# Four instead of two blocks of a depthwise convolution on TensorE, as products of 32 channels by four shifts

## The chip, the cores and the metric

The kernel runs on one core of a Trainium2 chip. The metric is the device time of one execution in microseconds (us). Engines are named as in the profile: PE is TensorE's matmul, PEld its weight load, DVE is VectorE, ACT is ScalarE, POOL is GpSimd, SP is SyncE, which issues most transfers.

## The reference, cut to what matters

The reference is a network of 256 tokens by 1024 features in f32: two layers of one block, then two of another. The change touches one mixer of the second block. It projects the tokens to several parts. One part goes through a gate and a causal depthwise convolution of 31 taps over 1024 channels, followed by a layer norm and SiLU; the other part is a state-space product (four-tap convolution, decays, chunked products). Both results are joined and projected.

```python
def conformer_conv(u, w_dw, b_dw, ln_g, ln_b):
    val, gate = jnp.split(u, 2, axis=-1)
    hid = causal_depthwise_conv(val * jax.nn.sigmoid(gate), w_dw, b_dw)   # 31 taps, each channel by itself
    return jax.nn.silu(layer_norm(hid, ln_g, ln_b))

def conv_ssd_mixer(u, w_in, ...):
    proj = u @ w_in
    conv_in, z, xbc, dt_raw = jnp.split(proj, [s0, s1, s2], axis=-1)
    ya = conformer_conv(conv_in, ...)
    yb = mamba2_ssd(z, xbc, dt_raw, ...)
    return jnp.concatenate([ya, yb], axis=-1) @ w_out
```

## The kernel before

Every weight is loaded in units of up to 1 MB by SP into `wr` (or `wxr`). ACT copies it to a rounded half `wh` (L225) and DVE subtracts to get the rest `wl` (L226), 1024 columns at a time. A product of f32 accuracy is three PE products, `wh` by high and low activations and `wl` by high ones (`mm3`, all on L206).

The mixer is `ssm`. Channels lie on partitions: 1024 channels are 8 blocks `f` of 128, and `hp` (named `glu` in the profile) holds for each block 30 zero columns and 256 tokens. `glu_turn(c)` transposes the gated values of blocks 2c and 2c+1 into `hp` and appends their convolutions as tasks.

- `taps(f)`: one ACT instruction (L1728) and 30 DVE instructions (L1730), each of which multiplies a shifted window of 256 columns by a channel's tap and adds it to `hc` (`hcv`). Six blocks go this way, in the queue `conv`.
- `taps_pe(f)`: blocks 1 and 6, in the queue `pconv`. ACT makes a diagonal matrix of 128 by 128 for each tap from the identity (`cdg`, by the copy on L222). PE multiplies each diagonal by the shifted window and sums all 31 in one PSUM tile (`cvq`, L206). One ACT instruction (L1756) adds the bias.

Meanwhile the projections run: `pj` of the parts `c` of xbc, of `glu` and of the gate `zz`. After each half of a weight product, `tick()` advances the queues `conv` and `ssd` by 1.4 steps and `pconv` by 0.65. What is posted there is emitted between the products; a scheduler then settles each engine's order. In `ssd`, `xbc_turn` transposes a block (`xbt`), has POOL zero three columns of a tile `xp` (L1870), copies the block into it on ACT, and runs a four-tap convolution: ACT's scaled copy (L1859) and three DVE instructions (L1861), then SiLU (L1862). `state` scales the results for the state product `stp` (`xdt`, `ssy`, `xds` on DVE). Then come the eight quads of the chunked product (`seg`, `yp`, `yo`). When `ssd` and `pconv` have been drained, `tp` transposes the state-space result, and the output projection `po` begins with that half. The layer norm of the convolution (`mu`, `var`) runs beside it, and the second half of `po` follows.

Small tiles come from pools of fixed size that are reused in turn: `t2` has 8 buffers and `a8` has 12. POOL has no transfer in this kernel; SP and ACT issue all. The modulation at the start (`ada`) is the one place where PE multiplies into quarters: 128 rows by 32 columns, output partitions 0, 32, 64 and 96 in turn, 512 columns each.

Of the kernel before, what the change touches and what calls it, by code (L numbers as in the profile page):

```python
# [11 lines left out]
F32 = mybir.dt.float32  # L12
# [3 lines left out]
OP = mybir.AluOpType  # L16
# [19 lines left out]
def shape_constants():  # L36
    p = np.arange(128)
    cm = np.zeros((128, C_N), np.float32)
    cm[:, C_ID:C_ID + 128] = np.eye(128)
    cm[:, C_TRI:C_TRI + 128] = p[:, None] <= p[None, :]  # L40
    cm[:, C_AFTER:C_AFTER + 128] = p[:, None] > p[None, :]
    cm[:, C_BEFORE:C_BEFORE + 128] = p[:, None] < p[None, :]
    cm[:, C_IOTA:C_IOTA + 128] = p[None, :]
    cq = p % 64
    ck = np.arange(64)
    c0 = np.clip(cq - 8, 0, 48)[:, None]
    cm[:, C_COL:C_COL + 64] = np.where((ck >= c0) & (ck < c0 + 16), 0.0, NEG)
    e = np.arange(8)
    cm[:, C_TIE:C_TIE + 64] = (e[None, :] < e[:, None]).reshape(1, 64)
    od = np.zeros((128, 2, 384), np.float32)  # L50
    t = np.arange(256)
    pos = np.stack([t // 64, t % 64], -1).astype(np.float32)
    inv = (10000.0 ** (-np.arange(16, dtype=np.float32) / 16)).astype(np.float32)
    ang = pos[:, :, None] * inv
    cos, sin = np.cos(ang), np.sin(ang)
    ct = np.stack([cos, cos], 2).reshape(256, 64)
    st = np.stack([-sin, sin], 2).reshape(256, 64)
    for q in range(2):
        rel = t[None, :] - (p[:, None] + 128 * q)
        od[:, q, 0:256] = np.where(np.abs(rel) <= 128, 0.0, NEG)  # L60
        od[:, q, 256:320] = ct[q * 128:(q + 1) * 128]
        od[:, q, 320:384] = st[q * 128:(q + 1) * 128]
    dl = np.zeros((128, 1152), np.float32)
    off = 0
    for q in range(2):
        n = 128 * (q + 1)
        rel = (p[:, None] + 128 * q) - np.arange(n)[None, :]
        for dil, win in ((1, 128), (4, 512), (16, 2048)):
            ok = (rel >= 0) & (rel % dil == 0) & (rel <= win)
            dl[:, off:off + n] = np.where(ok, -rel, -1e33)  # L70
            off += n
    return cm, od.reshape(128, 768), dl
# [81 lines left out]
class Net:  # L154
# [1540 lines left out]
    def ssm(self, x, nxt):  # L1695
        nc, I = self.nc, self.I
        V = nc.vector
        w = I["hyb_w_in_2"][0]
        hp = [self.a8([128, 1536], F32, "glu%d" % i) for i in range(2)]
        cw, pr = hp[0][:, 1144:1392], hp[0][:, 1392:1440]  # L1700
        dks = hp[0][:, 1440:1536].rearrange("p (a b) -> p a b", a=3)
        hp = [t[:, 0:1144].rearrange("p (f t) -> p f t", f=4) for t in hp]
        for i, n in enumerate(("ssm_dt_bias_2", "ssm_a_log_2", "ssm_d_2")):
            nc.scalar.dma_start(pr[:, 16 * i:16 * i + 16], I[n].to_broadcast([128, 16]))
# [2 lines left out]
        taps_in = [self.rows_in([("conv_dw_w_2", (15 * i, 15 + 16 * i), 120 + 8 * i)], self.t2([128, 128], "vrow"))  # L1707
                   for i in range(2)]
        hc = self.a8([128, 8, 256], F32, "hcv")
        on_pe = (1,6)  # L1710
        for i in range(2):
            nc.gpsimd.memset(hp[i][:, :, 0:30], 0.0)
        conv, ssd = Side(1.4), Side(1.4)
        pconv = Side(0.65)
        self.sides = [conv, ssd, pconv]
# [19 lines left out]
        def taps_pe(f):  # L1735

            xx = hp[f // 4][:, f % 4]
            p = self.ps([128, 256], "cvq")

            def diags(j0):  # L1740
                dh = self.t2([128, 4, 128], "cdg")
                for j in range(j0, min(j0 + 4, 31)):
                    c = j * 8 + f
                    self.copy(dh[:, j - j0], self.ident, cw[:, c:c + 1])
                return dh

            nxt = diags(0)
            yield
            for j0 in range(0, 31, 4):
                dh = nxt  # L1750
                if j0 + 4 < 31:
                    nxt = diags(j0 + 4)
                for j in range(j0, min(j0 + 4, 31)):
                    self.mm(p, dh[:, j - j0], xx[:, j:j + 256], j == 0, j == 30)
                yield
            nc.scalar.activation(hc[:, f], p, AF.Identity, bias=self.v("conv_dw_b_2", 0, f))  # L1756
            yield

# [18 lines left out]
        def glu_turn(c, gl):  # L1777
            tp = self.ps([128, 2, 256], "glt")
            for f in range(2):
                for tt in range(2):  # L1780
                    self.tr(tp[:, f, tt * 128:(tt + 1) * 128], gl[tt][:, f * 128:(f + 1) * 128])
            f0 = 2 * c % 4
            self.copy(hp[c // 2][:, f0:f0 + 2, 30:286], tp)
            for f in (2 * c, 2 * c + 1):
                if f in on_pe:
                    pconv.tasks.append(taps_pe(f))
                else:
                    conv.tasks.append(taps(f))
# [17 lines left out]
        p = self.ps([16, 256], "dtp")  # L1806
# [4 lines left out]
        p = self.ps([128, 2, 16], "dtt")  # L1811
# [12 lines left out]
        s = self.sm(32, "ssz")  # L1824
# [85 lines left out]
        for c in (2, 0, 1):  # L1910
            us = self.wunits(lambda r0, r1: [(w[r0:r1, 3072 + c * 512:3584 + c * 512], 512)])
            xb = []
            for tt in range(2):
                p = self.ps([128, 512], "pj")
# [76 lines left out]
        for c in range(2):  # L1991
            us = self.wunits(lambda r0, r1: [(w[r0:r1, 2048 + c * 512:2560 + c * 512], 512)])
            for tt in range(2):
                p = self.ps([128, 512], "pj")
# [218 lines left out]
def build(inputs, stop=None):  # L2213
    import concourse.bacc as bacc
    nc = bacc.Bacc("TRN2", target_bir_lowering=False, num_devices=1)
    arrays, args = {}, {}
    consts = dict(zip(("k_cm", "k_od", "k_dl"), shape_constants()))
    col = np.arange(64)
    rel = np.clip(col[None, :] - col[:, None] + 15, 0, 30)
    consts["k_rpb"] = np.asarray(inputs["ev_rpb"])[0][:, 4:11][:, :, rel].transpose(0, 2, 1, 3)  # L2220
    for name in [n for n in _INS if n != "ev_rpb"] + list(consts):
        a = np.ascontiguousarray(inputs[name] if name in inputs else consts[name])
        arrays[f"in_{name}_dram"] = a
        args[name] = nc.dram_tensor(f"in_{name}_dram", a.shape, mybir.dt.from_np(a.dtype), kind="ExternalInput").ap()
    out = nc.dram_tensor("out_0_dram", (1, 256, 1024), F32, kind="ExternalOutput").ap()
    with tile.TileContext(nc) as tc:
        with ExitStack() as ctx:
            Net(ctx, tc, args, out, stop).run()
    return nc, arrays
# [7 lines left out]
```

## Time and profile before

| | us |
|---|---|
| runs (three) | 2501.82, 2499.31, 2494.11 |
| median | 2499.31 |
| profiled execution, its own time | 2498.09 |
| its span, first to last instruction | 2496.3 |
| mean granted PE clock | 0.984 |
| PE busy | 2383.6 (95%) |
| DVE busy | 1812.5 (73%) |
| ACT busy | 1299.0 (52%) |
| POOL busy | 13.0 (1%) |

The profiled execution is one run of the program; its span leaves out 1.8 us around it. Matmuls are pipelined: a record lasts longer than the distance to the next, so what a product costs is the distance between starts. An f32 product leaves two records in the profile. The mixer's part that is touched runs from about 1500 to 1757 us.

### The profile page before, as it was taken

The numbers are of one execution on the slowest core, as the hardware profiler recorded it, in microseconds if no ns is written. First come the engines' busy times: TensorE is split into PE (matmuls) and PEld (weight loads), VectorE is DVE, ScalarE is ACT, GpSimd is POOL, SyncE is SP. The second block draws the span as 40 slices with busy tenths as digits, with TensorE's granted clock in tenths as the row PEclk, the third lists the DMA queues.
The fourth block names the chain that finished last, engine by engine and source line by source line (L and its number), as shares of the span: only waits on it lengthen the run. The fifth ranks groups of instructions, "written<-read, shape, count | busy, mean of one in ns | idle before, by whom it ended". The sixth has DMA issues, their size and how long they took to land.

```text
span 2496.3 us, 32333 instructions
## 1 busy us (share of the span) xinstructions
PE 2383.6 (95%) x11882; PEld 1981.9 (79%) x11882; DVE 1812.5 (73%) x3515; ACT 1299.0 (52%) x2230; POOL 13.0 (1%) x27
## 2 busy tenths in 40 slices
PE   7999999999899879999999999989999999999998
PEld 5878888888788658787877887877788788898886
DVE  5798988676686778989988556998744754646644
ACT  4445333232454568777776445775644544655533
POOL 0000000000000000000000000000000000000000
PEclk9999999999998999999999999999999999999999
DMA  8344455654221159999997654333665555554561
GB/s 275 115 133 163 152 186 190 215 163 166 75 81 56 55 170 321 331 324 338 313 352 264 194 189 144 102 102 126 220 199 172 186 185 167 146 153 136 191 196 51
DMA packets 381471, 455.15 MB, mean 182 GB/s; under 512 B 16680, under 2 KB 313337, under 8 KB 381305
## 3 DMA queue, kind: packets, MB, share of 16 engines
q1 hardware_dynamic: 375481, 445.86, 55.1%
q10 hardware_dynamic: 5824, 7.15, 0.9%
q8 instruction: 95, 1.56, 0.3%
q14 instruction: 71, 0.58, 0.1%
HBM read 451.91 MB, written 1.05 MB: 181 GB/s over the span
## 4 chain that ended last, share of the span: by engine, by line
PE 51%; DVE 7%; ACT 2%; DMA 2%; issue 1%; DVEq 0%; SPq 0%; ACTq 0%
PE gu L206 26%; PE acc L206 13%; PE pj L206 6%; DVE wl L226 3%; DMA wxr<-in_moe_w_dram 1%; DVE hcv L1730 1%; PE ht L209 1%; PE cvq L206 1%; PE po L206 1%; ACT wh L225 1%; PE oat L206 1%; DVE wxl L226 0%; PE mgp L206 0%; DVE c L1861 0%; PE pT L209 0%
## 5 line engine op out<-in xcount | busy, mean ns | idle before, releaser
L226 DVE TENSOR_TENSOR wl<-wr,wh 128x1024 fp32r<-128x1024 f32 (+1 forms) x510 | 590.9, 1186 | 168.7 <-ACT wh L225 167.7
L225 ACT ACTIVATE wh<-wr 128x1024 fp32r<-128x1024 f32 (+1 forms) x510 | 503.3, 1025 | 284.2 <-PE gu L206 55.9
L226 DVE TENSOR_TENSOR wl<-wxr,wh 128x1024 fp32r<-128x1024 f32 (+1 forms) x122 | 144.2, 1207 | 49.6 <-ACT wh L225 44.9
L566 DVE SCALAR_TENSOR_TENSOR aacc<-wr,sc,aacc 128x512 f32<-128x512 f32 x224 | 162.0, 761 | 14.6 <-DMA wr<-in_ada_w_dram 13.6
L206 PE MATMUL gu<-wh,xh 128*128 128x512 f32 x416 | 163.8, 394 | 2.6 <-ACT xh L229 2.6
L206 PE MATMUL gu<-wh,xl 128*128 128x512 f32 x416 | 162.9, 392 | 0.7 <-DVE xl L230 0.7
L206 PE MATMUL gu<-wl,xh 128*128 128x512 f32 x416 | 162.5, 391 | 0.0
L206 PE MATMUL gu<-wl,mgh 128*128 128x512 f32 (+1 forms) x384 | 146.3, 381 | 8.1 <-DVE wl L226 8.1
L225 ACT ACTIVATE wh<-wxr 128x1024 fp32r<-128x1024 f32 (+1 forms) x122 | 123.7, 1043 | 54.2 <-PE acc L206 13.9
L206 PE MATMUL gu<-wh,mgh 128*128 128x512 f32 (+1 forms) x384 | 144.9, 377 | 1.3 <-ACT wh L225 1.2
L226 DVE TENSOR_TENSOR wxl<-wr,wxh 128x1024 fp32r<-128x1024 f32 (+1 forms) x94 | 110.0, 1182 | 46.8 <-ACT wxh L225 43.7
L206 PE MATMUL gu<-wh,mgl 128*128 128x512 f32 (+1 forms) x384 | 143.1, 373 | 0.6 <-DVE mgl L226 0.6
L206 PE MATMUL acc<-wh,hid 128*128 128x512 f32 x416 | 135.3, 396 | 0.0
L435 ACT ACTIVATE sg<-gu,ry 128x256 f32<-128x256 f32 x88 | 41.2, 472 | 164.0 <-PE gu L206 158.8
L225 ACT ACTIVATE wxh<-wr 128x1024 fp32r<-128x1024 f32 (+1 forms) x94 | 95.0, 1024 | 43.4 <-PE acc L206 20.2
L436 DVE SCALAR_TENSOR_TENSOR sg<-gu,ry,sg 128x256 f32<-128x256 f32 x88 | 42.0, 480 | 103.8 <-ACT sg L435 103.8
L206 PE MATMUL acc<-wh,hh 128*128 128x512 f32 x352 | 115.9, 399 | 1.1 <-ACT wh L225 1.1
L206 PE MATMUL gu<-wxh,xh 128*128 128x512 f32 x288 | 113.6, 395 | 1.7 <-ACT xh L229 1.6
L206 PE MATMUL gu<-wxh,xl 128*128 128x512 f32 x288 | 113.2, 393 | 1.4 <-DVE ri L286 0.8
L206 PE MATMUL gu<-wxl,xh 128*128 128x512 f32 x288 | 113.0, 392 | 0.0
L206 PE MATMUL pj<-wh,xh 128*128 128x512 f32 (+1 forms) x248 | 96.9, 392 | 0.6 <-ACT xh L229 0.6
L206 PEld LDWEIGHTS gu<-wh,xh 128*128 128x128 f32 x416 | 78.3, 188 | 20.5 <-ACT xh L229 4.7
(548 smaller groups left out, 5847.0 us busy)
## 6 DMA issues: line engine op xcount, KB each, us to landing
wr<-in_ffn_w_dram SPq DMA_DIRECT2D x176, 512.0 KB
wr<-in_moe_w_dram SPq DMA_DIRECT2D x124, 512.0 KB
wr<-in_ffn_w_dram SPq DMA_DIRECT2D x45, 1024.0 KB
wr<-in_ada_w_dram SPq DMA_DIRECT2D x42, 1024.0 KB
wr<-in_moe_w_dram SPq DMA_DIRECT2D x28, 1024.0 KB
wxr<-in_ffn_w_dram SPq DMA_DIRECT2D x44, 512.0 KB
wxr<-in_moe_w_dram SPq DMA_DIRECT2D x40, 512.0 KB
wr<-in_attn_w_qkv_dram SPq DMA_DIRECT2D x54, 256.0 KB
```

What stands on the lines that cost most here:

```text
L206: self.nc.tensor.matmul(out, lhsT, rhs, start=start, stop=stop)
L209: self.nc.tensor.transpose(out, in_, self.ident)
L225: self.nc.scalar.activation(h, src, AF.Copy)
L226: self.split_op = self.nc.vector.tensor_sub(l, src, h.bitcast(F32))
L435: nc.scalar.activation(g, p[:, 0:n], AF.Silu, scale=rs[tt])
L436: nc.vector.scalar_tensor_tensor(g, p[:, n:2 * n], rs[tt], g, op0=OP.mult, op1=OP.mult)
L566: self.nc.vector.scalar_tensor_tensor(a[:, s], w, col, a[:, s], op0=OP.mult, op1=OP.add)
L1730: V.scalar_tensor_tensor(a, xx[:, j:j + 256], tap(j), a, op0=OP.mult, op1=OP.add)
```

## The change

Blocks 1, 3, 6 and 7 go to PE, and each in another form. A block of 128 channels is cut into four groups `g` of 32 channels. A tile `shifted` (`cxs`) of 128 partitions by 4 groups by 284 columns holds, for group g, the 32 channels four times, shifted by 0, 1, 2 and 3 columns. It is filled by 16 transfers on chip of 32 partitions each, issued by POOL: 64 for the four blocks. A product then takes 128 partitions, which are 32 channels by 4 shifts, and 32 output columns into a quarter of the PSUM tile. Eight products (`r`) with windows 4 columns apart make 32 taps, the last one zero; 4 groups by 8 are 32 products a block. The weights `cdg` come from the taps, laid out on the host as `k_cw`, by two POOL products a block instead of ACT's copies. There is one `shifted` tile for all four blocks.

```diff
+        cq = hp[1][:, 1144:1432]
+        nc.scalar.dma_start(cq, I["k_cw"])
...
-        on_pe = (1,6)
+        on_pe = (1, 3, 6, 7)
         for i in range(2):
             nc.gpsimd.memset(hp[i][:, :, 0:30], 0.0)
+        shifted = self.a8([128, 4, 284], F32, "cxs")
+        nc.gpsimd.memset(shifted[:, :, 283:284], 0.0)
...
             xx = hp[f // 4][:, f % 4]
+            eye = cq[:, None, 256:288].to_broadcast([128, 16, 32])
+            dw = [self.t2([128, 4, 4, 32], "cdg") for _ in range(2)]
+            for i in range(2):
+                c = f * 32 + i * 16
+                nc.gpsimd.tensor_tensor(dw[i].rearrange("p r g c -> p (r g) c"), eye,
+                                        cq[:, c:c + 16, None].to_broadcast([128, 16, 32]), op=OP.mult)
+            for s in range(4):
+                for g in range(4):
+                    n = 284 if s < 3 else 283
+                    nc.gpsimd.dma_start(shifted[32 * s:32 * s + 32, g, 0:n], xx[32 * g:32 * g + 32, s:s + n])
+            for _ in range(6):
+                yield
             p = self.ps([128, 256], "cvq")
-
-            def diags(j0):
...
-            for j0 in range(0, 31, 4):
-                dh = nxt
-                if j0 + 4 < 31:
-                    nxt = diags(j0 + 4)
-                for j in range(j0, min(j0 + 4, 31)):
-                    self.mm(p, dh[:, j - j0], xx[:, j:j + 256], j == 0, j == 30)
-                yield
+            for r in range(8):
+                for g in range(4):
+                    self.mm(p[32 * g:32 * g + 32], dw[r // 4][:, r % 4, g], shifted[:, g, 4 * r:4 * r + 256], r == 0, r == 7)
+                if r % 2:
+                    yield
```

The change also moves instructions. POOL first, from the two memsets of `hp` on; `glu_17573` is `hp[0]` and `glu_17574` is `hp[1]`, which also holds the taps. Before:

```order
L1520 COMPARE_AND_BRANCH
L1520 UNCONDITIONAL_BRANCH x2
L1712 MEMSET glu_17573 128x4x30
L1712 MEMSET glu_17574 128x4x30
L1870 MEMSET xp 128x3 x12
```

After (lines are two to four higher):

```order
L1716 MEMSET cxs 128x4
L1746 TENSOR_TENSOR cdg<-glu_17574 128x512 x2
L1751 DMA cxs<-glu_17573 32x284 x12
L1751 DMA cxs<-glu_17573 32x283 x4
L1874 MEMSET xp 128x3 x9
L1751 DMA cxs<-glu_17573 32x284 x2
L1874 MEMSET xp 128x3
L1751 DMA cxs<-glu_17573 32x284 x10
L1751 DMA cxs<-glu_17573 32x283 x4
L1874 MEMSET xp 128x3 x2
L1746 TENSOR_TENSOR cdg<-glu_17574 128x512 x2
L1751 DMA cxs<-glu_17574 32x284 x2
```

All twelve `xp` memsets stand behind block 1's 16 transfers, one of them also behind two of block 3's and two behind all of block 3's; the transfers of blocks 6 and 7 follow.

PE, from the last quads of the state-space part to the output projection. Before:

```order
L206 MATMUL yo<-st,bcT 128x512
L206 MATMUL yp<-xdt,mm 128x64 x4
L206 MATMUL cvq<-glu_17574,cdg 128x256 x4
L206 MATMUL yp<-xdt,mm 128x64 x4
L206 MATMUL yo<-st,bcT 128x512
L206 MATMUL cvq<-glu_17574,cdg 128x256 x19
L209 MATMUL tp<-cm,xs 128x128 x16
L206 MATMUL po<-wh,ybh 128x512
```

After:

```order
L206 MATMUL yo<-st,bcT 128x512
L206 MATMUL yp<-xdt,mm 128x64 x4
L206 MATMUL cvq<-cxs,cdg 32x256 x8
L206 MATMUL yp<-xdt,mm 128x64 x4
L206 MATMUL yo<-st,bcT 128x512
L206 MATMUL cvq<-cxs,cdg 32x256 x59
L209 MATMUL tp<-cm,xs 128x128 x2
L206 MATMUL cvq<-cxs,cdg 32x256 x29
L209 MATMUL tp<-cm,xs 128x128 x14
L206 MATMUL po<-wh,ybh 128x512
```

All 96 products of blocks 3, 6 and 7 (8, 59 and 29) have come to stand here; block 1's 32 stand between the projections earlier.

## Rows read from the trace of the kernel before

**Rows 1.** The page: busy time by engine, and the chain's shares.

```profile
PE 2383.6 (95%) x11882; PEld 1981.9 (79%) x11882; DVE 1812.5 (73%) x3515; ACT 1299.0 (52%) x2230; POOL 13.0 (1%) x27
...
PE 51%; DVE 7%; ACT 2%; DMA 2%; issue 1%; DVEq 0%; SPq 0%; ACTq 0%
```

**Rows 2.** Stretches (from:to, length): busy by engine, granted PE clock, DMA share, GB/s.

```profile
1560.00:1570.00 10.00, 10.00 (x52) 8.41 (x51) 9.12 (x25) 8.69 (x16) 0.20 (x2) 1.00 0.06 9
...
1630.00:1640.00 10.00, 4.38 (x10) 2.00 (x8) 10.00 (x22) 3.70 (x7) 0.00 (x0) 0.83 0.00 1
...
1690.00:1700.00 10.00, 6.79 (x25) 5.64 (x25) 10.00 (x34) 5.72 (x19) 0.00 (x0) 0.83 0.19 59
```

**Rows 3.** Timeline of PE: start, length, instructions [idle before, and what ended it].

```profile
1589.14 0.38 PE L209 MATMUL xbt<-cm,xb 128*128 128x128 f32 x2
...
1636.63 2.05 PE L206 MATMUL stp<-xds,btm 128*128 128x512 f32 x2 [5.62 <-DVE xds L1895]
1637.69 1.42 PE L206 MATMUL pj<-wh,xh 128*128 128x512 f32 x1
1638.90 1.37 PE L206 MATMUL stp<-xds,btm 128*128 128x512 f32 x2
```

**Rows 4.** Timeline of PE at the last convolution products of block 6.

```profile
1688.11 1.89 PE L206 MATMUL cvq<-glu,cdg 128*128 128x256 f32 x8
1693.21 8.43 PE L206 MATMUL cvq<-glu,cdg 128*128 128x256 f32 x30 [3.21 <-ACT cdg L222]
1701.48 1.91 PE L209 MATMUL tp<-cm,xs 128*128 128x128 f32 x16
```

**Rows 5.** Instructions of the tile `cdg`: count, ns min/median/max, first and last start.

```profile
L206 PE MATMUL cvq<-glu,cdg x124: 377/379/631, 1567.4 to 1701.3; 128*128 128x256 f32 x124
L222 ACT ACTIVATE cdg<-cm,glu x62: 384/387/401, 1554.7 to 1696.9; 128x128 f32<-128x128 f32 x62
```

**Rows 6.** Timeline of PE in the modulation at the start.

```profile
38.73 3.64 PE L206 MATMUL ada<-adw,scw 128*32 128x512 f32 x32
```

**Rows 7.** Timeline of DVE: taps of one block, back to back.

```profile
1568.06 3.65 DVE L1730 SCALAR_TENSOR_TENSOR hcv<-glu,hcv 128x256 f32<-128x256 f32 x9
```

**Rows 8.** Timeline of POOL, three of its instructions.

```profile
2.69 0.23 POOL L516 TENSOR_TENSOR sel<-cm 128x2 f32<-128x2 f32 x1 [1.65 <-DMA cm<-in_k_cm_dram]
...
56.13 2.39 POOL L863 TENSOR_TENSOR bias<-bias,cm 128x1024 f32<-128x1024 f32 x1 [49.77 <-DMA bias<-in_k_rpb_dram]
...
1561.20 0.10 POOL L1870 MEMSET xp<- 128x3 f32 x1 [59.75 <-PE glt L209]
```

**Rows 9.** Timeline of DVE around POOL's product of 56.13.

```profile
55.23 0.94 DVE L226 TENSOR_TENSOR wl<-wr,wh 128x768 fp32r<-128x768 f32 x1
...
56.42 2.91 DVE L226 TENSOR_TENSOR wl<-wr,wh 128x768 fp32r<-128x768 f32 x1
```

**Rows 10.** Timeline of SP: time that issuing a transfer took (64, 24 and 1024 KB).

```profile
0.74 0.39 SPq L319 DMA_DIRECT2D cm<-in_k_cm_dram  x1
...
18.35 1.30 SPq L354 DMA_DIRECT2D vrow<-in_ada_b_dram  x1
...
1525.57 0.37 SPq L254 DMA_DIRECT2D wxr<-in_hyb_w_in_dram  x1
```

**Rows 11.** Timeline of ACT at the first blocks' copies and the first `xp`.

```profile
1561.43 0.59 ACT L222 ACTIVATE glu<-glt 128x512 f32<-128x512 f32 x1
...
1572.89 0.51 ACT L1859 ACTIVATE c<-xp,vec 128x256 f32<-128x256 f32 x1
...
1574.59 1.28 ACT L1862 ACT_TABLE_LOAD   x1
...
1579.93 1.06 ACT L225 ACTIVATE wh<-wxr 128x1024 fp32r<-128x1024 f32 x1 [1.18 <-PE pj L206]
```

**Rows 12.** The chain in order of time: start, length, what.

```profile
1574.11 2.79 PE pj L206 x12
```

More of the change, by code (lines that the diff above doesn't have):

```diff
@@ L1737, in taps_pe @@
             xx = hp[f // 4][:, f % 4]
-            p = self.ps([128, 256], "cvq")
-            def diags(j0):
-                dh = self.t2([128, 4, 128], "cdg")
-                for j in range(j0, min(j0 + 4, 31)):
[L1743 to L1747, printed above, removed]
-            yield
-            for j0 in range(0, 31, 4):
-                dh = nxt
-                if j0 + 4 < 31:
-                    nxt = diags(j0 + 4)
-                for j in range(j0, min(j0 + 4, 31)):
-                    self.mm(p, dh[:, j - j0], xx[:, j:j + 256], j == 0, j == 30)
-                yield
+            eye = cq[:, None, 256:288].to_broadcast([128, 16, 32])
[10 more added lines that the diff above has]
+                yield
+            p = self.ps([128, 256], "cvq")
+            for r in range(8):
[3 more added lines that the diff above has]
+                    yield
             nc.scalar.activation(hc[:, f], p, AF.Identity, bias=self.v("conv_dw_b_2", 0, f))
@@ L2219, in build @@
     rel = np.clip(col[None, :] - col[:, None] + 15, 0, 30)
+    taps = np.zeros((32, 1024), np.float32)
+    taps[0:31] = np.asarray(inputs["conv_dw_w_2"])[0]
+    consts["k_cw"] = np.concatenate([taps.reshape(8, 4, 8, 4, 32).transpose(1, 4, 2, 0, 3).reshape(128, 256),
+                                     np.tile(np.eye(32, dtype=np.float32), (4, 1))], 1)
     consts["k_rpb"] = np.asarray(inputs["ev_rpb"])[0][:, 4:11][:, :, rel].transpose(0, 2, 1, 3)
```

## The prediction

> **What bounds the kernel now.** I read the first part of the page and its chain of waits first [rows 1]: TensorE (PE) is busy for 95% of the span and carries 51% of the chain. Any stretch is therefore priced by asking when PE gets through it. The change touches one mixer, so I took the stretch table of 1560 to 1702 us next [rows 2]. There VectorE (DVE) is as full as PE. Between 1630 and 1640 us PE runs only 4.38 of 10 us, and between 1690 and 1700 us only 6.79. The timeline of PE names both gaps. A state product waits 5.62 us for DVE's `xds` [rows 3], and the last convolution products wait 3.21 us for ScalarE's (ACT's) diagonals [rows 4]. Each gap also costs clock. After the second one, 30 products take 8.43 us, while 8 take 1.89 us before it (0.216 us from one to the next, so 30 would take 6.6) [rows 4]. A wait thus costs about 1.8 us beyond itself, and the granted clock of those stretches is 0.83 instead of 1.00 [rows 2], the mean of a part at 1.2 GHz after the idle time and the rest at 2.4.
>
> **The change, part by part.**
>
> *PE.* Before, two blocks issue 124 records [rows 5] at 0.216 us, which is 27 us. After, four blocks of 32 products issue 256 records (an f32 product leaves two). A row of the same form is in the trace: the modulation products `ada`, 128 rows by 32 columns into four quarters in turn, 32 records of 512 columns in 3.64 us [rows 6], or 0.107 us each after the fill. At 256 columns that is half, 0.0535 us, so 256 records are 13.7 us. PE gives up **13.3 us**.
>
> *The two old gaps.* Block 3's and block 7's 60 taps leave DVE. Nine taps take 3.65 us [rows 7], so they are 60 x 0.40 = 24 us. The 62 diagonals leave ACT [rows 5]. With them go the 5.62 us and the 3.21 us, and a clock loss of 1.8 us each (less for the first, whose products run only some 3 us at the low clock, 1.6): **12.2 us** at most, nothing at least. I take all of it, since the engine that was late loses more work than the gap.
>
> *GpSimd's (POOL's) eight diagonal products.* They are new there and DVE feels them. While POOL's two-input product of 1024 columns runs 2.39 us from 56.13 [rows 8], DVE's subtraction of 768 columns takes 2.91 us instead of 0.94 [rows 9]. This is what the Trainium skill, "SBUF — State Buffer", section "SBUF: two separate sides", states: a GpSimd operation and a VectorE operation that reads two SBUF inputs exclude each other for a whole instruction. By that rule, and the trace agrees, eight products of half that size (1.2 to 1.3 us) take up to 10 of the 24 us back from DVE. That leaves 14, still more than the gap.
>
> *The 64 transfers.* They are the price that decides. They go through POOL's queue, and the order shows three facts. POOL waits with a block's transfers until the block before has been multiplied, because there is one `shifted` tile. The multiplications of blocks 3, 6 and 7 stand in one run at the end of the state-space part, before the output projection. And the twelve small `xp` memsets of POOL, 0.10 us each [rows 8], now stand behind transfers.
>
> No row shows a transfer issued by POOL. SP takes 0.37 us for one of 1 MB and 1.30 us for a small one of 48 rows, 24 KB [rows 10]. Those are my two ends, 0.37 and 1.30 us. By rows, 32 of 48 make 0.87 of the dear one. Each of these transfers also waits for a semaphore that the eighth before it used. I take **1.0 us**, nearest to the dear row. The Trainium skill, "DMA: Bandwidth & Descriptors", section "Latency and other measured facts", names about 1 us for the first byte of a GpSimd transfer; by that price the sum would be the one below. Landing: the first constant is issued at 0.74 us and POOL gets it at 2.69 us [rows 8, 10], 1.6 us after its issue ended. I take 2.0, since weights share the engines.
>
> *First new wait.* Block 1's transfers can start when ACT has copied its rows, at 1562.0 us [rows 11]. Sixteen end at 1578.0, and the first `xp` memset runs then. ACT would reach the scaled copy that needs it near 1571.4 (1572.89 before [rows 11], less one group of convolution products ahead on PE). ACT is in order: behind that copy stand the copies out of PSUM and the weight halves `wh`. From 1578.0 it needs about 8.1 us to the copy `xb` that PE's next transposes read (four scaled copies, a table load of 1.28 and two halves of 1.06 [rows 11], the other copies at 0.3 to 0.7). PE had those transposes at 1589.14 [rows 3]; four groups earlier, at 1.7 us each, is 1582.4. PE waits about **4 us**.
>
> *Second.* When block 1 has been multiplied, block 3's 16 transfers start. One memset stands behind the first two, and two behind all sixteen. The first costs PE 1.5 us. By the last, PE has 46 projection products ahead, 10.7 us at 0.233 [rows 12]. ACT needs 2.5 us behind the memset, so 16 + 2.5 - 1.5 - 10.7 = **6.3 us**. Together the new waits are 12 us; at 0.37 us a transfer they are 1, at 1.30 they are 21.
>
> *The tail.* Block 3's products are the last that have their data when PE gets to them. Block 6's 16 transfers follow them, with two diagonal products of 1.3 us in the same queue: 16 + 2.6 + 2.0 = 20.6 us. Then PE multiplies, and block 7's transfers follow: 16 + 2.0 = 18.0 us. Nothing is queued on PE that could go ahead; the transposes for the output projection stand behind. **38.6 us** (18.4 at 0.37; 48.2 at 1.30), and 2 x 1.8 = 3.6 us of clock after the two waits.
>
> *The sum* is -13.3 - 12.2 + 12 + 38.6 + 3.6 = +28.7 us. The profiled execution took 2498.1 us, 1.2 below the median of the runs. That gives 2526.8 us, **2527**. The norm of the convolution and the output projection behind the tail are PE-bound before, so the shift passes through them.
>
> **The rivals.**
>
> *A cheap issue: not slower.* If POOL issues as quickly as SP issues its weights, 0.37 us, the memsets come in time and the tail shrinks to 18.4 us. The sum is -13.3 - 12.2 + 1 + 18.4 + 3.6 = -2.5 us, 2495.6. For it speaks that SP's rows are mostly the cheap ones; against it, that SP's small transfer is the dear one. The point at which this becomes "no change" is 0.65 us a transfer (sum +7.5). The Trainium skill, "DMA: Bandwidth & Descriptors", section "Issuing engines are not separate DMA queues", says that initiating a DMA is usually small relative to the DMA itself. By that rule this rival holds; no run here shows it yet for POOL. Faster than 2491 needs under 0.28 us, or more gaps of PE closed than the two.
>
> *A dear issue.* Past 1.30 us, or with landing slower than 2.0 us under the weights' traffic, the result is 2545 to 2550 and beyond: the sum at 1.30 is -13.3 - 12.2 + 21 + 48.2 + 3.6 = +47.3. For it: POOL writes the transfers itself while DVE excludes it at times [rows 9].
>
> *The quarters don't overlap: the change doesn't do what it says.* If a product of 32 columns takes PE as long as one of 128, 256 records at 0.216 are 55 us, 42 more than summed: 2568. Against it stands the row of `ada` [rows 6].
>
> **How the numbers follow.** Forecast 2527, with an issue of 0.65 to 1.3 us: 0.64. Cheap issue: 0.18, of which 0.04 reach faster. Dear issue: 0.13. No overlap: 0.05. From the cheap bound, 2496, to the dear one with slow landing, 2550, some 2 in 10 are left out. A measurement of this kernel tells 0.3%, 7.5 us, from no change. Faster is 0.04, the same 0.14, slower 0.82.
>
> **What would show it.** In the profile after, POOL's queue should show 64 transfers in four runs of 16, each 12 to 18 us long, and the stretch of 1560 to 1700 should be near 28 us longer. PE should have two idle gaps of 18 to 21 us with only the products of block 6 between them, waiting for DMA, and the granted clock should fall after each. ACT's scaled copies of `xp` should wait for POOL. The 8-record groups of `cvq` should take near 0.43 us. It is wrong if the transfers take under 0.65 us, if the two gaps are under 10 us, or if PE's waits sit elsewhere than before `cvq`.

## The result, and the profile after

The changed kernel takes 2514.8 us (median), the kernel before 2497.1 (median of five runs, the three of the table above among them). The medians differ by 17.7 us; the ratio is 1.0061, 95% interval 1.0046 to 1.0076, or 15 us more. The forecast was 2527, slower, in a range of 2496 to 2550. The sign held. The price on which the prediction let it hang did not: a transfer takes half of what was assumed, and other terms made up part of the difference.

The profiled execution spans 2513.3 us, 17.0 more than before. Two points of TensorE's (PE's) timeline cut this up: the transposition `dtt` at the mixer's start, and the transposition `tp` of `res` behind the output projection. Before, they stand at 1554.85 and 1754.83 us, 199.98 apart. After:

```profile
1553.53 0.29 PE L1817 MATMUL dtt<-cm,dtr 16*128 16x16 f32 x2 [0.46 <-ACT dtr L222]
...
1767.06 1.03 PE L209 MATMUL tp<-cm,res 128*128 128x128 f32 x8
```

That is 213.53 apart: **the mixer costs 13.5 us more**. Ahead of it 1.3 us were gained, and behind it 4.7 lost (746.2 instead of 741.5 to the end), both with unchanged work. The loss behind sits in one place, some 530 us behind the mixer, where the same products run at a lower granted clock. First the stretches of before, then of after, which lie 13 us later (columns as in [rows 2], the clock third from the end):

```profile
2280.00:2290.00 10.00, 9.48 (x65) 8.67 (x64) 3.05 (x6) 3.92 (x12) 0.00 (x0) 0.93 0.57 212
2290.00:2300.00 10.00, 9.95 (x47) 7.63 (x45) 6.42 (x18) 5.73 (x14) 0.00 (x0) 1.00 0.00 1
```

```profile
2290.00:2300.00 10.00, 8.91 (x46) 8.51 (x47) 4.58 (x7) 5.29 (x14) 0.00 (x0) 0.61 0.59 205
2300.00:2310.00 10.00, 9.48 (x37) 7.93 (x37) 1.00 (x3) 1.08 (x4) 0.00 (x0) 0.70 0.17 54
```

The other profiles below fall on either side too, 740.8 to 741.5 or 746.0 to 747.0 us behind the mixer, whatever they change. So single profiles are compared by their mixer stretch here, and kernels by their medians.

Now the mixer. Busy times on the page, which answer to [rows 1]: POOL has gone from 13.0 to 57.9 us, PE is as busy as before, although its products are cheaper.

```profile
PE 2383.9 (95%) x12014; PEld 1975.0 (79%) x12014; DVE 1790.1 (71%) x3455; ACT 1281.3 (51%) x2168; POOL 57.9 (2%) x100
```

The stretches that answer to [rows 2]:

```profile
1630.00:1640.00 10.00, 8.88 (x46) 7.14 (x45) 9.93 (x19) 5.98 (x13) 0.00 (x0) 1.00 0.58 211
...
1660.00:1670.00 10.00, 10.00 (x54) 9.17 (x54) 8.00 (x15) 6.00 (x13) 0.00 (x0) 0.79 0.03 10
...
1680.00:1690.00 10.00, 0.00 (x0) 0.00 (x0) 7.78 (x19) 1.59 (x5) 8.69 (x15) 0.73 0.85 247
1690.00:1700.00 10.00, 7.16 (x64) 3.51 (x64) 0.00 (x0) 0.17 (x1) 3.85 (x6) 0.58 0.10 23
```

PE's timeline at the places of [rows 3, 4]:

```profile
1626.74 1.12 PE L206 MATMUL stp<-xds,btm 128*128 128x512 f32 x2 [1.42 <-ACT btm L222]
...
1656.77 1.81 PE L206 MATMUL seg<-cm,lt 128*128 128x128 f32 x8 [2.53 <-ACT lt L222]
...
1677.01 2.80 PE L206 MATMUL cvq<-cxs,cdg 128*32 128x256 f32 x48
1692.63 7.16 PE L206 MATMUL cvq<-cxs,cdg 128*32 128x256 f32 x64 [12.82 <-DMA cxs<-glu]
1707.52 2.01 PE L206 MATMUL cvq<-cxs,cdg 128*32 128x256 f32 x6 [7.73 <-DMA cxs<-glu]
1709.46 0.69 PE L209 MATMUL tp<-cm,xs 128*128 128x128 f32 x2
1710.08 4.57 PE L206 MATMUL cvq<-cxs,cdg 128*32 128x256 f32 x58
1714.58 1.75 PE L209 MATMUL tp<-cm,xs 128*128 128x128 f32 x14
```

The reader is to see four things. The state product comes 10 us earlier than in [rows 3] (8.6 if counted from `dtt`), and its gap is 1.42 instead of 5.62. From `dtt` to the end of the last `yo` PE needs 123.6 us instead of 133.4, so it enters the tail 9.9 us ahead. Then two gaps, 12.82 and 7.73 us, are followed by products at half speed: the 64 records of block 6 take 7.16 us, where 48 take 2.80 just before. And a wait that the prediction did not name, 2.53 us for ACT's `lt`, is followed by a granted clock of 0.79. The kernel before waited for `lt` too, in two shorter waits, with a granted clock of 1.00 from 1640 to 1660:

```profile
1648.24 0.49 PE L206 MATMUL seg<-cm,lt 128*128 128x128 f32 x2 [1.53 <-ACT lt L222]
...
1658.01 0.49 PE L206 MATMUL seg<-cm,lt 128*128 128x128 f32 x2 [1.08 <-ACT lt L222]
```

What POOL does in the tail, and the row of its 64 transfers (issue time, minimum/median/maximum):

```profile
1680.36 1.03 POOL L1751 DMA_DIRECT2D cxs<-glu  x2 [60.49 <-issue]
1681.41 2.06 POOL L1746 TENSOR_TENSOR cdg<-glu 128x512 f32<-128x512 f32 x2
1683.40 5.67 POOL L1751 DMA_DIRECT2D cxs<-glu  x11
1691.28 1.47 POOL L1751 DMA_DIRECT2D cxs<-glu  x3 [2.21 <-DMA cxs<-glu]
...
1699.67 7.93 POOL L1751 DMA_DIRECT2D cxs<-glu  x16 [4.85 <-PE cvq L206]
```

```profile
L1751 POOL DMA_DIRECT2D cxs<-glu x64: 496/496/677, 1561.4 to 1707.1; - x64
...
DMA to landing us min/median/max: 1.7/1.7/6.1
```

A transfer takes **0.50 us** to issue, not 1.0. It has landed 1.7 us after its issue began, but up to 6.1 while weights fill the DMA engines (share 0.85 from 1680 to 1690): there POOL waits 2.21 us for a transfer before it can issue three more.

### The profile page after: what moved, and what is told of

It reads as the page before. It is cut to its first block, busy times and chain, and to the rows that moved or that the text cites. A ratio compares the mean times of both kernels' runs of the same rounds, so it can differ in the third digit from the quotient of the medians.

```text
span 2513.3 us, 32590 instructions
## 1 busy us (share of the span) xinstructions
PE 2383.9 (95%) x12014; PEld 1975.0 (79%) x12014; DVE 1790.1 (71%) x3455; ACT 1281.3 (51%) x2168; POOL 57.9 (2%) x100
## 3 DMA queue, kind: packets, MB, share of 16 engines
HBM read 452.06 MB, written 1.05 MB: 180 GB/s over the span
## 4 chain that ended last, share of the span: by engine, by line
PE 49%; DVE 7%; issue 4%; DMA 2%; ACT 2%; POOL 1%; SPq 0%; DVEq 0%; ACTq 0%; POOLq 0%
PE gu L206 26%; PE acc L206 12%; PE pj L206 5%; DVE wl L226 3%; PE po L206 2%; PE ht L209 1%; DVE hcv L1734 1%; DMA wr<-in_moe_w_dram 1%; PE oat L206 1%; DMA wxr<-in_moe_w_dram 1%; ACT wh L225 1%; DVE c L1865 1%; POOL cxs L1751 0%; PE mgp L206 0%; DVE wxl L226 0%
## 5 line engine op out<-in xcount | busy, mean ns | idle before, releaser
L566 DVE SCALAR_TENSOR_TENSOR aacc<-wr,sc,aacc 128x512 f32<-128x512 f32 x224 | 160.1, 752 | 14.5 <-DMA wr<-in_ada_w_dram 13.5
L225 ACT ACTIVATE wxh<-wr 128x1024 fp32r<-128x1024 f32 (+1 forms) x94 | 95.0, 1024 | 43.5 <-PE acc L206 20.3
```

The lines of the kernel that those rows point to most:

```text
L225: self.nc.scalar.activation(h, src, AF.Copy)
L566: self.nc.vector.scalar_tensor_tensor(a[:, s], w, col, a[:, s], op0=OP.mult, op1=OP.add)
```

## The experiments

The theory: block 6's and block 7's transfers each begin only when the block before has left the one `shifted` tile, and at that point PE has nothing else queued. The rivals: the transfers, the diagonal products or their queue cost wherever they stand; the loss sits ahead of the tail; or the products are slow by themselves. "Mixer" is from `dtt` to `tp` of `res`, "tail" from the end of the last `yo` to the first `po`, both of the profiled execution; the ratio is to the kernel before, timed on the same chip.

| kernel | median us | ratio [95%] | mixer | tail |
|---|---|---|---|---|
| before | 2497.1 | | 199.98 | 14.9 |
| changed | 2514.8 | 1.0061 [1.0046, 1.0076] | 213.53 | 39.0 |
| no_transfers_6_7 | 2482.4 | 0.9943 [0.9921, 0.9966] | 187.53 | 11.3 |
| two_tiles | 2498.9 | 1.0007 [0.9995, 1.0019] | 202.58 | 28.0 |
| three_tiles | 2478.2 | 0.9916 [0.9898, 0.9933] | 182.63 | 14.5 |
| early_products | 2493.7 | 0.9992 [0.9980, 1.0004] | 194.62 | 9.9 |
| split_transfers | 2526.9 | 1.0119 [1.0088, 1.0150] | 228.84 | 50.7 |
| issue_from_sp | 2512.7 | 1.0063 [1.0043, 1.0083] | 214.47 | 39.9 |
| keep_warm | 2521.5 | 1.0097 [1.0073, 1.0120] | 225.14 | 50.6 |
| keep_warm_sized | 2506.9 | 1.0034 [1.0017, 1.0050] | 210.23 | 35.7 |
| po_first | 2506.4 | 1.0044 [1.0023, 1.0065] | 211.89 | 12.7 |
| lt_on_pool | 2514.8 | 1.0070 [1.0047, 1.0094] | 214.30 | 37.8 |
| two_blocks | 2498.4 | 1.0000 [0.9988, 1.0011] | 206.10 | 12.0 |

### Do the transfers of blocks 6 and 7 cost it?

```diff
             for s in range(4):
                 for g in range(4):
                     n = 284 if s < 3 else 283
-                    nc.gpsimd.dma_start(shifted[...], xx[...])
+                    if f < 4:
+                        nc.gpsimd.dma_start(shifted[...], xx[...])
```

> Leaves out the transfers of blocks 6 and 7; their products read what block 3 left in the tile. Everything else is the same, GpSimd's diagonal products included. Theory: the gaps of 12.82 and 7.73 us go, and the products of both blocks run at full clock (3.5 us each instead of 7.16 and 6.6): PE reaches the output projection near 1689.5 instead of 1716.1, 2488 (2484 to 2493). So all that the change gains elsewhere shows by itself: 9 us against the kernel before. Rival (the slowdown sits elsewhere, in the waits for VectorE and ScalarE before 1680 us or behind 1716 us): 2500 or more.

Measured 2482.4, below the expectation, and a mixer 26.0 us shorter than the changed kernel's. PE's timeline has all three blocks in one piece, 0.055 us a record:

```profile
1673.20 9.70 PE L206 MATMUL cvq<-cxs,cdg 128*32 128x256 f32 x176
```

So the loss is in these 32 transfers and what follows on them. Without them the change is worth 12.5 us in the mixer.

### Is it the one tile?

```diff
-        shifted = self.a8([128, 4, 284], F32, "cxs")
+        shifts = [self.a8([128, 4, 284], F32, "cxs%d" % i) for i in range(2)]
...
+            shifted = shifts[on_pe.index(f) % 2]
```

> Two shifted tiles in turn instead of one; the order on TensorE (PE) is unchanged. Theory (the single tile makes the transfers of blocks 6 and 7 serial): block 6's transfers run near 1640 us, long before they are needed, so the gap of 12.82 us and the half clock after it (7.16 - 3.6) go, 16.4 us; block 7's transfers still wait for block 3's products, so the gap ahead of them grows from 7.73 to about 10 us. 14 us less than the changed kernel: 2501 (2497 to 2505). Rival (PE is late for GpSimd's diagonal products or for the weights' traffic, not for the tile): the gap stays, 2515.

Measured 2498.9, as expected, and no different from the kernel before (the interval holds 1). The gap ahead of block 6 is down to 2.42 us and waits for its diagonals; the one ahead of block 7, which still shares block 3's tile, has grown to 9.71:

```profile
1678.17 3.97 PE L206 MATMUL cvq<-cxs,cdg 128*32 128x256 f32 x64 [2.42 <-POOL cdg L1748]
1691.86 1.39 PE L206 MATMUL cvq<-cxs,cdg 128*32 128x256 f32 x6 [9.71 <-DMA cxs<-glu]
```

Then three tiles, with `range(3)` and `% 3`, so that no transfer waits for a late block.

> Three shifted tiles: blocks 1 and 7 share one, blocks 3 and 6 have their own; all 64 transfers stay. On GpSimd the transfers of blocks 6 and 7 then stand behind the last xp memset, near 1640 us, with the quads beside them, and PE's order ends with 88 products in a row. Theory (only the wait for the tile costs): both gaps go, up to 3 us come back where the diagonal products of blocks 6 and 7 wait for a small tile: 2486 (2482 to 2492), below the kernel before and near the run without these transfers (2482.4). Rival (32 transfers in a row beside the weights' traffic and the quads cost as much elsewhere): 2497 or more.

Measured **2478.2 us, 0.84% faster than before**, with all 64 transfers in place. POOL issues blocks 6 and 7 from 1637 us on, beside the quads, and PE goes through its products without a gap:

```profile
1637.05 4.43 POOL L1753 DMA_DIRECT2D cxs<-glu  x9 [16.44 <-ACT lt L222]
...
1654.30 2.93 POOL L1753 DMA_DIRECT2D cxs<-glu  x6 [0.27 <-DMA cxs<-glu]
```

```profile
1657.57 0.49 PE L206 MATMUL seg<-cm,lt 128*128 128x128 f32 x2 [0.97 <-ACT lt L222]
...
1674.41 9.70 PE L206 MATMUL cvq<-cxs,cdg 128*32 128x256 f32 x176
1686.04 1.09 PE L209 MATMUL tp<-cm,xs 128*128 128x128 f32 x8 [1.92 <-DVE xs L132]
```

The tail is 24.5 us shorter than the changed kernel's. Another 6.4 us go ahead of it, from `dtt` to the last `yo` (117.2 instead of 123.6): the wait of 2.53 us for `lt` and the low clock after it are not there. These 6.4 us are not a wait for the tile. The scheduler also settled another order on ACT. In the changed kernel ACT turns from the quads to the gate `zz` and back just ahead of the late `lt` of 1656.33, and each turn loads another function table, 1.28 us:

```profile
1652.47 1.28 ACT L2000 ACT_TABLE_LOAD   x1
1653.83 0.69 ACT L2000 ACTIVATE zz<-pj,ry 128x512 f32<-128x512 f32 x1
1654.54 1.28 ACT L1952 ACT_TABLE_LOAD   x1
```

With three tiles the `zz` stand behind the quads, ACT loads no table between the first `mm` of the quads and the last (four in the changed kernel), and the whole program has 12 table loads instead of 16:

```profile
1666.93 1.28 ACT L2002 ACT_TABLE_LOAD   x1
```

No run has this order with one tile, so the share of the loads is read from the two traces and not tested by itself. The profiled mixer is 17.4 us shorter than before's; the rest of the 21 us that the ratio gives is not seen there.

### Or the order of the products?

`pconv = Side(0.65)` becomes `Side(2.0)`, with one tile.

> One number: the convolution tasks on PE advance at 2.0 steps per half of a weight product instead of 0.65; still one shifted tile and 64 transfers. Block 3's products then stand between the projections and block 6's between the quads, so each block's transfers have other PE work beside them. Theory (what costs is that the transfers of two blocks lie behind the last work of PE, not that there are 64 of them): both gaps and their half clock go, PE gets to the transposes near 1687 instead of 1714 us: 2488 (2484 to 2495), below the kernel before. At most 2 us come back where block 1's first products reach PE before its transfers have landed. Rival (GpSimd's queue and its lock on VectorE cost wherever they stand): the waits move ahead, 2505 to 2515.

Measured 2493.7, above the 2488 and within the range, but not clear of the kernel before (the interval holds 1); the tail is the shortest of all, with waits of 0.69 and 0.86 us for transfers. But PE now also waits 3.0 us for them ahead of the tail, and the products stand in smaller groups there: from `dtt` to the last `yo` it takes 134.1 us, 10.5 more than the changed kernel, where the 112 records that have moved ahead of it would be 6.2 at 0.055. Moving the products takes the tail away, but not for nothing; another tile does it better.

The other way round, the output projection's first half goes ahead of the waiting products:

```diff
-        pconv.drain()
         for tt in range(2):
             yb.b(tt)
...
-        conv.tasks.append(norm())
-        conv.rate = 3
+        pconv.tasks.append(norm())
+        pconv.rate = 3
```

> One shifted tile and all transfers as in the changed kernel, but the convolution tasks of PE need not be finished before the transposes and the output projection: its first half is put ahead of and between the products of blocks 6 and 7, and the norm follows them. Theory (the gaps cost because nothing that PE could do stands ahead of them): the waits fill with output products, the half clock goes too: 2489 (2484 to 2497). Rival (the norm, which needs blocks 6 and 7, comes so much later that the second half of the projection waits for it): 2500 or more.

Measured 2506.4, so the rival's bound held. The gaps for transfers have gone (0.33 us are left), and two others stand in their place, on the norm of the convolution and on the transposes' input. PE's waits from 1650 to 1770 us:

```profile
PE po L206 <- ACT yah L225: 7.3, 1, 7.3
PE tp L209 <- DVE rt L301: 6.3, 1, 6.3
```

### What does a transfer cost?

Each is cut into two of half the columns, the same bytes in all.

> Each transfer on chip is cut into two of half the columns, same bytes: 128 instead of 64. Theory (the issue of 0.50 us in GpSimd's queue is the price): a block's run grows from 8 to 16 us, the two tail gaps by 8 us each, and the early waits that the prediction worked out at 1.0 us a transfer appear, up to 12 us: 2531 to 2543. That is the prediction's price of 16 us a block put to the test; its own sum was 2527. Rival (the bytes or the landing set the time): 2515.

Measured 2526.9, some 4 us under the theory's lower end and 12 above the rival. The issue stays at 0.496 us for half the bytes, so a block's run doubles and the gaps become 18.67 and 13.86:

```profile
1706.33 6.79 PE L206 MATMUL cvq<-cxs,cdg 128*32 128x256 f32 x64 [18.67 <-DMA cxs<-glu]
1726.98 2.00 PE L206 MATMUL cvq<-cxs,cdg 128*32 128x256 f32 x4 [13.86 <-DMA cxs<-glu]
```

```profile
L1752 POOL DMA_DIRECT2D cxs<-glu x128: 496/496/698, 1565.3 to 1728.2; - x128
```

This is the prediction's own case, 16 us a block, and the mixer is 28.9 us longer than before, where it summed 28.7. That the sums agree is partly luck. The gaps are 32.5 instead of 38.6, and the early waits far less than 12: from `dtt` to the last `yo` the split costs 3.6 us. ACT's timeline shows why. It does wait for the `xp` memset, but only 2.31 us, since the scheduler put two weight halves ahead of the waiting copy, and ACT stood 5.37 us waiting for PE before those:

```profile
1579.36 2.01 ACT L225 ACTIVATE wh<-wxr 128x1024 fp32r<-128x1024 f32 x2 [5.37 <-PE pj L206]
1583.68 0.51 ACT L1864 ACTIVATE c<-xp,vec 128x256 f32<-128x256 f32 x1 [2.31 <-POOL xp L1875]
```

Then SP issues the transfers instead of POOL (`nc.sync` for `nc.gpsimd`).

> The 64 transfers are issued by SP, between the weights' loads, instead of GpSimd; one shifted tile, PE's order unchanged. It prices the issue on the queue whose rows the prediction took its ends from (0.37 and 1.30 us). If SP takes 0.37 us for each, a block's run is 5.9 instead of 8 us and the two gaps shrink by 2 us each: 2510 (2507 to 2513). If a small one costs 1.30 there, a run is 20.8 us and the gaps grow by 12.8 each: 2540. Rival: SP stands at block 1's products before it can go on to block 3's transfers, and the weights behind them come late, so the waits move to the projections: above 2520 with gaps that are shorter than 12.8 and 7.7.

Measured 2512.7, at the upper end of the first case's range, but not by its price. A transfer takes 0.59 us there at the median and a block 10 to 11 us, neither of the two ends of [rows 10], and the gaps are 12.80 and 9.40 us. The rival's waits did not come: from `dtt` to the last `yo` it takes 123.6 us, as in the changed kernel. The row of the 64 transfers:

```profile
L1751 SPq DMA_DIRECT2D cxs<-glu x64: 507/588/1450, 1557.2 to 1705.1; - x64
```

### What does the low clock cost?

```diff
+            if f > 5:
+                d = self.ps([128, 512], "dum")
+                n = 28 if f == 6 else 17
+                for i in range(n):
+                    self.mm(d, self.ident, xdt[:, 0, 0:512], i == 0, i == n - 1)
             p = self.ps([128, 256], "cvq")
```

> Adds 28 and 17 idle products (128x512, f32, into a tile that nobody reads) on PE ahead of the products of blocks 6 and 7, so that PE is busy while it would wait for the transfers. Theory (the half clock after each wait costs 7.16 - 3.5 and 6.6 - 3.4, nearly 7 us in all, where the prediction had 3.6): the products of both blocks take 3.5 us each, 2508 (2505 to 2512). Rival (the rate of these products in the tail is not the clock's but that of their quarters or of the landing): no change, 2515.

Measured 2521.5: a miss of mine. One idle product takes 0.868 us (two records), so they overran the gaps by 18.6 us. But both blocks' products run in 3.66 us behind them:

```profile
1674.41 24.30 PE L206 MATMUL dum<-xdt,cm 128*128 128x512 f32 x56
1698.64 3.66 PE L206 MATMUL cvq<-cxs,cdg 128*32 128x256 f32 x64
1702.23 14.86 PE L206 MATMUL dum<-xdt,cm 128*128 128x512 f32 x34
1717.02 3.66 PE L206 MATMUL cvq<-cxs,cdg 128*32 128x256 f32 x64
```

With 14 and 9 of them:

> The idle products again, fitted to the two waits: in keep_warm one of them took 0.868 us, so 28 and 17 filled 39.2 us where 20.6 were to fill; now 14 and 9, 12.2 and 7.8 us. Theory: in keep_warm both blocks' products took 3.66 us instead of 7.16 and 6.6, so with a fill that doesn't overrun the stretch from the last yo to the output projection is some 6 us shorter than the changed kernel's 39.0, and the time 2509 (2505 to 2512). Rival (idle products delay the next transfers as much as they save): 2514 or more.

Measured 2506.9, as expected for the whole, but the tail is only 3.3 us shorter than the changed kernel's, not 6. Block 6 still takes 5.15 us after a wait of 0.37 us; block 7 is at full speed. In sum: at full speed the two blocks take 7.3 us, in the changed kernel 7.16 and 6.4 (from 1707.52 to 1714.58 less the transposes' 0.69). The low clock costs 6.3 us.

### What else holds PE?

The quads' copies `lt` go to POOL (`nc.gpsimd.tensor_scalar` for ACT's copy).

> The 32 scaled copies lt of the quads go from ScalarE (ACT) to GpSimd, which is idle there. Theory (with the two old gaps gone ACT is late next, in the quads: 2.5 us of wait and 3.7 us of half clock that the prediction did not name): up to 6 us less than the changed kernel, 2509. Rival (ACT is not the cause, or GpSimd takes longer for four copies than ACT's 1.27 us): 2515 or more.

Measured 2514.8, no gain. The wait of 2.53 us falls to 0.66, and others for POOL's copies come, 1.25 us the longest:

```profile
1641.53 0.49 PE L206 MATMUL seg<-cm,lt 128*128 128x128 f32 x2 [1.25 <-POOL lt L1949]
...
1659.69 2.23 PE L206 MATMUL seg<-cm,lt 128*128 128x128 f32 x8 [0.66 <-POOL lt L1949]
```

In sum PE waits 3.4 us for `lt`, where it waited 3.6. By itself the run doesn't settle whether ACT's load is the cause there; the traces of the changed kernel and of three tiles, compared above, point to the table loads. Last, only blocks 1 and 6 in the new form, `on_pe = (1, 6)`.

> Only blocks 1 and 6 on PE, as before, but in the new form; blocks 3 and 7 go back to VectorE (DVE). Theory: block 6's transfers wait for block 1's products, long done, so no gap in the tail. PE saves some 17 us and the gap for the diagonals with its clock, 5; but DVE still carries its 60 taps more, so the gap ahead of the state product grows from 5.6 to about 14: 2484 (2478 to 2492). Rival (what counts is the 24 us that DVE loses): DVE ends last in the tail and the time stays at 2497.

Measured 2498.4: the rival. The tail has no gap for a transfer, but VectorE's (DVE's) taps last until 1718 us, and PE waits for DVE and then for the norm. Its waits from 1684 to 1759 us:

```profile
PE po L206 <- ACT yah L225: 4.9, 1, 4.9
PE tp L209 <- DVE xs L132: 3.1, 1, 3.1
```

The cheaper products alone are worth nothing that can be measured here (the profiled mixer is even 6.1 us longer than before's, and the medians show no difference). So what pays, by comparison with no_transfers_6_7 and three_tiles, is that two blocks leave DVE.

## Why the prediction was right in sign and off in size

**Where it was right.** The mechanism is the one it named: one tile, the products of three blocks at the end, nothing to go ahead. Two gaps stand ahead of `cvq` with only block 6's products between them, they wait for DMA, and the clock falls after each. Three tiles, which take the wait for the tile away, turn 15 us lost into 21 gained; 6.4 us of this lie ahead of the tail and came with the other order on ACT.

**The step that failed** is the price of a transfer. "I take 1.0 us, nearest to the dear row" leaned on SP's issue of 48 rows [rows 10]; POOL takes 0.50, whatever the bytes. The cheap rival's condition, under 0.65 us, was met, and its result did not come; the forecast's own, 0.65 to 1.3 us, was not. At 0.50 the prediction's own steps give no early wait, a tail of 8 + 2.6 + 2.0 + 8 + 2.0 = 22.6 us and a sum of +0.7. The mixer measured +13.5. So that "slower" came out is in part luck: with the right price the same working forecasts no change, and what made the kernel slower all the same are terms that it sized too low or did not name. Of its own signs of being wrong, one came (transfers under 0.65 us) and one by half (the second gap, 7.73 us, is under 10). The rest, term by term:

| term | predicted | at 0.50 us | measured |
|---|---|---|---|
| PE's products | -13.3 | -13.3 | -9.8 |
| the two old gaps with their clock | -12.2 | -12.2 | -10.8 |
| early waits | +12 | 0 | +2.4 |
| quads: waits and low clock | not named | | +4.5 |
| the two tail gaps | +38.6 | +22.6 | +20.6 |
| low clock after them | +3.6 | +3.6 | +6.3 |
| all else on PE, no item above 0.7 | not named | | +0.3 |
| sum | +28.7 | +0.7 | +13.5 |

- *PE's products.* In one run 176 records take 9.70 us, 0.055 each, near the 0.0535 taken from [rows 6]. In groups of 6 to 16 between other products, 80 records took 5.5 us from start to start, 0.069 each. All 256 took 22.0 us, or 15.7 without the low clock below, not 13.7. The 124 records of before took 27.3 us from start to start, or 25.5 without the 1.8 us of low clock, not 27.
- *The old gaps.* 5.62 us became 1.42, with its products at full clock; the 3.21 us for the diagonals [rows 4] and the clock after them have gone.
- *Early waits.* PE waits 1.9 us for `xsT`, 0.6 for `wl` and 0.3 for `tg`, where before it waited 0.4 for `xsT`. At double the issue time the stretch up to the last `yo` grew by 3.6 us, not by the 12 that the working gives: the working took ACT's order of before for granted.
- *The quads.* "The engine that was late loses more work than the gap" was right for DVE. But PE already waited for ACT's `lt`, 2.6 us in all, and with DVE and the diagonals out of the way it waits 3.6 (1.11 and 2.53). The `seg` products behind the longer wait take 1.81 us for 8 records; at full clock, ten us later, 8 take 1.05. With their waits, `seg` and `yp` take 20.4 us from start to start instead of 15.9. The prediction asked what is late next only for the tail.
- *The tail gaps* were sized by the price alone. The landing of 2.0 us, counted from the end of an issue, was 1.2 in an idle stretch and up to 5.6 beside the weights. And a product needs only the four transfers of its group: PE takes up block 7 at 1707.52, before the sixteenth issue ends at 1707.60, so that gap is 7.73 us and not 8 + 2.0.
- *The low clock* was carried over from a gap of 3.21 us with 30 products behind it. Here 128 records stood behind two longer gaps, nearly all of them at half speed.

**POOL's diagonals and DVE.** The prediction gave them up to 10 us of DVE's time. DVE lost about 3.5 us: 2.2 in one `wl` (3.44 instead of 1.22), and 0.6 to 0.7 each in two others. POOL lost about 4.8: its eight products take 1.04 us at best, one takes 1.48 and one 5.38 while DVE subtracts.

```profile
L1746 POOL TENSOR_TENSOR cdg<-glu x8: 1044/1054/5376, 1550.3 to 1693.8; 128x512 f32<-128x512 f32 x8
```

```profile
1681.11 3.44 DVE L226 TENSOR_TENSOR wl<-wr,wh 128x1024 fp32r<-128x1024 f32 x1
```

The Trainium skill, "SBUF — State Buffer", section "SBUF: two separate sides", states that whichever of the two starts first has the shared ports for its whole instruction. The trace agrees in part. A `wl` that begins 0.24 us behind POOL's product of 1550.34 takes 1.89 us instead of 1.22, and POOL's product of 5.38 us stands beside four `wl` of 1.21 each. But the `wl` of 1681.11 is recorded 0.30 us ahead of POOL's product and lost all the same; POOL was issuing transfers until just before, and why it came first is open.

**The rule behind the cheap rival.** The row first: 16 issues of 0.50 us are 8.0 us, against 1.7 us from the start of one issue to its landing. The Trainium skill, "DMA: Bandwidth & Descriptors", section "Issuing engines are not separate DMA queues", says that initiating is usually small relative to the DMA itself. For one transfer of 36 KB the row agrees; for 16 in a row behind one wait the issue is the larger part.

## What to carry to other kernels

Before pricing a transfer on chip, ask when its target is free and what its reader's engine can do meanwhile: one buffer for four users in turn made 32 cheap transfers cost 26 us, and two more buffers made the same change 0.84% faster than before, 6.4 us of it ahead of the tail, where another order of ScalarE's instructions came with them. Where many small transfers wait for one event, count the issues and not the bytes. And when a change takes work from the engine that was late, follow the bound engine on to the waits that it still has, with the clock that they cost, not only to the place where the change adds one.

## What the runs showed of the hardware

- POOL issues a transfer on chip in 0.496 us, for 32 partitions of 284 columns as for 142; SP in 0.59 us at the median for the same ones.
- Such a transfer from POOL has landed 1.7 us after its issue began on idle queues, and up to 6.1 us after that at a DMA share of 0.85.
- A turn of ScalarE from the quads to the gate and back loads two function tables, 1.28 us each.
- After a wait of 12.8 us PE's products of block 6 took 7.16 us in a stretch of granted clock 0.58, near the lower of its two levels (1.2 GHz); behind products without a gap the same ones took 3.66.
- What lies behind the mixer, the same in all kernels, ran some 5 us longer in 6 of 13 profiles; in the changed kernel's, 20 us of it ran at a granted clock of 0.61 and 0.70. A difference of that size between two single profiles says nothing.
